# Gate recurrence between the first two heads, the first half of a modulation on TensorE, lambda first, and routing's GpSimd work on VectorE

## Chip, core and metric

One core of a Trainium2 chip runs the whole kernel. The metric is the device time of one execution in microseconds (us). The engines are named PE (TensorE, matmul), PEld (its weight loads), DVE (VectorE), ACT (ScalarE), POOL (GpSimd) and SP (SyncE, which issues most DMAs). SBUF and PSUM are the on-chip memories; P is 128, the number of partitions.

## What is computed

One decoder block for 512 tokens of width 1024, all float32. Cut to what the change touches:

```python
mod = silu(c) @ ada_w + ada_b                      # 1024 -> 6144
sh1, sc1, gt1, sh2, sc2, gt2 = split(mod, 6)
h = rmsnorm(x, norm1_w) * (1 + sc1) + sh1
qa, ka, va, qm, km, vm, om, ip, fp, ga, gm = split_cols(h @ w_in)
lam = exp(sum(lam_q1 * lam_k1)) - exp(sum(lam_q2 * lam_k2)) + lam_init
y_a = diff_attention(qa, ka, va, lam, subln_w)     # 8 heads, softmax(a) - lam * softmax(b)
hm  = mlstm_chunkwise(qm, km, vm, ip, fp)          # gates ip, fp: a recurrence over 8 chunks of 64
x   = x + gt1 * ((sigmoid(ga) * y_a + sigmoid(gm) * rms(hm) * sigmoid(om)) @ w_out)
h2  = rmsnorm(x, norm2_w) * (1 + sc2) + sh2
# product-key routing: 8 heads, two lists of 128 keys each
v_top, i_top = top_k(scores, 16)                   # 16 of each list
cand = v_top[0][:, None] + v_top[1][None, :]       # sums of pairs
cand_idx = i_top[0][:, None] * 128 + i_top[1][None, :]
sc, sel = top_k(cand, 16); idx = cand_idx[sel]; gate = softmax(sc)
x = x + gt2 * sum_e gate_e * gelu(U[idx_e] . h2) * V[idx_e]   # 16384 experts
return rmsnorm(x, final_norm_w)
```

## The kernel before

The kernel is written in Python on a framework that puts each engine's instructions in a fixed order at build time; on the chip each engine runs its list in order, with semaphores between engines. Buffers come from pools with a fixed number of slots (`bufs`), and an instruction that wants a slot waits for its last reader. Products in float32 precision are made of three matmuls: an operand is split in a rounded part (hi, a cast on ACT) and a rest (lo, a subtraction on DVE or POOL).

1. **Start**, to about 70 us. `ada_early(half)` loads 16 tiles of `ada_w` (128x512) for each half of the columns of sh1 and sc1, and DVE adds each, times the condition vector, to an accumulator (`ada_step`, lines 217 and 219); `ada_cols` (line 224) sums it over the partitions with one-column matmuls against ones and adds the bias (line 225). sh1 and sc1 make hT (hi on ACT, line 291; lo on DVE, line 293), the input of all projections; the projections q and k of the first two heads and the gates are multiplied first (line 187 and below). Behind that stands the lambda chain (lp, ls, le, nl, psl).
2. **Heads**, to about 690 us. Four passes `hp` of two heads each: `attention(hp)` with two heads `u`, `mlstm(hp)`, and the gates om, gm, ga (line 682). In pass 0 `gate_chain()`, the recurrence over the forget gates on 8 partitions, stands behind `attention(0)`.
3. **Routing**, about 697 to 1005 us. For three of the four token tiles: `scores` and `top16` (lines 747 to 751), `select` (line 772: pair sums cand on DVE and cidx on POOL; per head a comparison eq, 128x800, on DVE, its product oh with cidx on POOL, the sum idxf on DVE), `slots` (transposes; expert index taken apart by shift and mask), and `build_w`: for each of 48 batches of 8 tokens two one-hot tensors n2T, n1T and two gated ones ghi, glo (line 844, 128x1024 f16 each), from which PE makes the dense weights W (wps, lines 852 and 853). Six of the 48 glo are made on POOL (`PLO`). Meanwhile the first experts' products `up(n1)` run ahead, by up to 32 (`NGA`): raw_U is loaded, hi_U cast on ACT (line 966), lo_U subtracted (line 967: POOL for n1 < 35, else DVE), a one-column copy `pace` on POOL (line 969) and 24 act matmuls of 128x384 (lines 975 to 977).
4. **Main loop**, about 1013 to 1960 us. n1 from 0 to 127, 128 experts in each: `up(n1)`, the load and split of V (hi_V, lo_V), ga times W (line 1006), its split ahi and alo, and 18 y matmuls of 128x512 (line 1021). The fourth token tile is routed inside this loop by `select_gather` (at n1 = 3 and 5) and served by indirect DMAs (gath) from POOL, with DVE adding up (lines 907 and 917).

Of the kernel before, what the change touches and what calls it, by code (L numbers as in the profile page):

```python
# [1108 lines left out]
```

## Time and profile before

| | us |
|---|---|
| median of 3 runs (1979.67 to 1980.06) | 1979.73 |
| the profiled execution, its own time | 1986.29 |
| its span in the trace | 1984.2 |
| PE busy | 1826.5 (92%) |
| DVE busy | 1465.3 (74%) |
| POOL busy | 861.2 (43%) |
| ACT busy | 806.8 (41%) |

The profile is of one execution; its busy times are of the whole span and average over stages that are unlike. Windows give the same by stage. Where an instruction is in a group, "idle before" is the time its engine stood still ahead of it, with the event that ended it.

### The profile page before, as it was taken

What the parts mean: (1) busy time and instruction counts of PE and PEld (TensorE: products, weight loads), DVE (VectorE), ACT (ScalarE), POOL (GpSimd) and SP (SyncE); (2) the same over time, 40 slices, a digit from 0 to 9 for tenths busy, and PEclk for the clock granted to TensorE, in tenths of its full rate; (3) what the DMA queues carried; (4) which work ended last, traced back from release to release, by engine and by line L of the source; (5) the groups of instructions that cost most, each with busy time, mean ns of one, the idle gap of its engine ahead of it and who ended that gap; (6) DMA issues with size and microseconds to landing.
All of it is one profiled execution on the core that took longest, in us unless ns stands there. A gap on an engine that the chain in (4) does not pass through costs nothing.

```text
span 1984.2 us, 29045 instructions
## 1 busy us (share of the span) xinstructions
PE 1826.5 (92%) x10748; PEld 1648.0 (83%) x10748; DVE 1465.3 (74%) x2740; ACT 806.8 (41%) x1361; POOL 861.2 (43%) x721
## 2 busy tenths in 40 slices
PE   5989999899997988778899989999999999999997
PEld 4979899798986877678888778889988888888986
DVE  7653646546557799998999878888777677767777
ACT  4545464464553323344444333333333333332332
POOL 2513425234234256675533556555433423333433
PEclk8999999999998999899899999999999999999998
DMA  7321414324223222255596699999978888887983
GB/s 278 123 64 60 149 65 154 113 67 139 64 86 107 86 90 81 85 183 202 203 312 215 216 331 339 334 345 348 337 253 296 293 283 291 288 299 234 320 290 129
DMA packets 160284, 404.27 MB, mean 204 GB/s; under 512 B 14471, under 2 KB 63368, under 8 KB 160142
## 3 DMA queue, kind: packets, MB, share of 16 engines
q1 hardware_dynamic: 117026, 240.91, 37.2%
q0 software_dynamic: 36864, 134.23, 18.6%
q10 hardware_dynamic: 6252, 27.28, 3.6%
q8 instruction: 84, 1.38, 0.3%
q14 instruction: 58, 0.48, 0.1%
HBM read 373.52 MB, written 28.84 MB: 203 GB/s over the span
## 4 chain that ended last, share of the span: by engine, by line
PE 51%; DVE 23%; DMA 10%; issue 6%; POOL 5%; ACT 4%; SPq 0%; DVEq 0%; POOLq 0%; ACTq 0%
PE y L1021 18%; PE act L977 5%; PE act L975 5%; PE act L976 5%; DMA ada_w<-ada_w 4%; DMA gath<-V,idx 3%; DVE onehot L844 3%; DVE gated L844 2%; DVE lo_V L138 1%; DVE lo_U L967 1%; DVE eq L797 1%; DMA gath<-U,idx 1%; POOL gath L901 1%; DVE idxf L800 1%; ACT hi_U L966 1%
## 5 line engine op out<-in xcount | busy, mean ns | idle before, releaser
L977 PE MATMUL act<-h_hi,lo_U 128*128 128x384 f32 x1024 | 353.9, 346 | 14.7 <-POOL lo_U L967 9.7
L975 PE MATMUL act<-h_hi,hi_U 128*128 128x384 f32 x1024 | 351.5, 343 | 1.9 <-ACT ga L979 1.9
L976 PE MATMUL act<-h_lo,hi_U 128*128 128x384 f32 x1024 | 350.7, 342 | 0.0
L917 DVE SCALAR_TENSOR_TENSOR yg<-gath,act,yg 128x1024 f32<-128x1024 f32 x127 | 162.9, 1283 | 110.3 <-DMA gath<-V,idx 109.6
L1021 PE MATMUL y<-lo_V,ahi 128*128 128x512 f32 x762 | 238.9, 394 | 5.5 <-DVE lo_V L138 5.5
L1021 PE MATMUL y<-hi_V,alo 128*128 128x512 f32 x762 | 234.1, 394 | 4.0 <-DVE alo L138 4.0
L1021 PE MATMUL y<-hi_V,ahi 128*128 128x512 f32 x762 | 222.1, 396 | 7.3 <-ACT hi_V L137 7.3
L901 POOL DMA_INDIRECT gath<-U,idx x128 | 176.6, 1380 | 115.3 <-DVE junk L907 101.1
L137 ACT CAST hi_V<-raw_V 128x1024 fp32r<-128x1024 f32 x128 | 134.1, 1051 | 225.6 <-PE y L1021 197.1
L977 PEld LDWEIGHTS act<-h_hi,lo_U 128*128 128x128 f32 x1024 | 197.0, 192 | 22.4 <-POOL lo_U L967 11.1
L969 POOL COPY pace<-lo_U 128x1 f32<-128x1 f32 x128 | 69.9, 548 | 331.6 <-DVE lo_U L967 330.1
L975 PEld LDWEIGHTS act<-h_hi,hi_U 128*128 128x128 f32 x1024 | 197.8, 193 | 10.8 <-ACT ga L979 3.1
L976 PEld LDWEIGHTS act<-h_lo,hi_U 128*128 128x128 f32 x1024 | 197.5, 193 | 3.6
L137 ACT CAST ahi<-ga 128x384 fp32r<-128x384 f32 x127 | 65.1, 513 | 302.2 <-DVE ga L1006 152.1
L138 DVE TENSOR_TENSOR lo_V<-raw_V,hi_V 128x1024 fp32r<-128x1024 f32 x128 | 158.0, 1236 | 33.2 <-ACT hi_V L137 30.6
L966 ACT CAST hi_U<-raw_U 128x1024 fp32r<-128x1024 f32 x128 | 134.1, 1048 | 110.0 <-PE act L976 92.3
L1021 PEld LDWEIGHTS y<-hi_V,alo 128*128 128x128 f32 x762 | 143.5, 189 | 35.9 <-DVE alo L138 5.2
L1021 PEld LDWEIGHTS y<-lo_V,ahi 128*128 128x128 f32 x762 | 142.7, 189 | 36.7 <-DVE lo_V L138 7.9
L1021 PEld LDWEIGHTS y<-hi_V,ahi 128*128 128x128 f32 x762 | 143.0, 190 | 32.1 <-ACT hi_V L137 8.0
L901 POOL DMA_INDIRECT gath<-V,idx x128 | 152.5, 1192 | 38.0 <-issue 30.2
L907 DVE SCALAR_TENSOR_TENSOR junk<-gath,hrow 128x1024 bf16<-128x1024 f32 x128 | 156.1, 1220 | 11.9 <-DMA gath<-U,idx 11.2
L967 POOL TENSOR_TENSOR lo_U<-raw_U,hi_U 128x1024 fp32r<-128x1024 f32 x35 | 105.0, 3001 | 72.5 <-ACT hi_U L966 59.1
(461 smaller groups left out, 4413.1 us busy)
## 6 DMA issues: line engine op xcount, KB each, us to landing
raw_U<-UT SPq DMA_DIRECT2D x128, 512.0 KB, 5.1
raw_V<-V SPq DMA_DIRECT2D x128, 512.0 KB, 5.0
ada_w<-ada_w SPq DMA_DIRECT2D x96, 256.0 KB, 4.0
W_dram<-st ACTq DMA_DIRECT2D x24, 960.0 KB, 4.5
...
```

The lines of the kernel that those rows point to most:

```text
L137: A.copy(hi, src)
L138: eng.tensor_tensor(lo, src, hi.bitcast(F32), op=OP.subtract)
L844: eng.tensor_tensor(dst.rearrange("p t (n u) -> p t n u", u=2), x.rearrange("p t (n u) -> p t n u", u=2), bc(y[:, b * TB:(b + 1) * TB, Non ...
L901: G.indirect_dma_start(out=t_, out_offset=None, in_=src, in_offset=bass.IndirectOffsetOnAxis(ap=idx0[:, s:s + 1], axis=0))
L907: V.scalar_tensor_tensor(junk2, u, 1.0, hrow, op0=OP.mult, op1=OP.mult, accum_out=act[:, s:s + 1])
L917: V.scalar_tensor_tensor(yg, v, act[:, s:s + 1], yg, op0=OP.mult, op1=OP.add)
L966: A.copy(hi, raw)
L967: (G if n1 < NGA + 3 else V).tensor_tensor(lo, raw, hi.bitcast(F32), op=OP.subtract)
L975: T.matmul(ps, hi[:, ks], h_hi[:, k], start=(k == 0), stop=False)
L976: T.matmul(ps, hi[:, ks], h_lo[:, k], start=False, stop=False)
L977: T.matmul(ps, lo[:, ks], h_hi[:, k], start=False, stop=(k == KD - 1))
L1021: T.matmul(ys[d][j], l[:, tsl], r[:, j * 512:(j + 1) * 512], start=(m == 0 and i == 0), stop=(m == KEYS - 1 and i == 2))
```

## The change

Five things change.

1. The 16 `ada_w` tiles of the first half are no longer multiplied on DVE; PE multiplies each (condition column as the stationary operand, one row of 512 results, added up in PSUM), ACT copies the row, and `ada_cols` then uses one row. The second half stays on DVE.
2. The lambda chain is written at the very start, and the load of its four vectors second in SP's queue.
3. `gate_chain` is called between the two heads of pass 0, not behind them.
4. `select` finds both key indices by comparing the position with the 16 offsets of the pair list, on DVE in f16 alone, for four heads in one instruction; POOL makes neither cidx nor oh, and `slots` needs no shift and mask. In `build_w` the two one-hot operations become one of 128x2048, and all glo are made on DVE.
5. lo_U is made on DVE always (line 967 before, 994 after).

```diff
+    def ada_cols(acc, n, b0, dst, rows=P):
...
-            T.matmul(ps[:, k:k + 1], acc[:, k * P:(k + 1) * P], ones[:, 0:1], start=True, stop=True)
+            T.matmul(ps[:, k:k + 1], acc[0:rows, k * P:(k + 1) * P], ones[0:rows, 0:1], start=True, stop=True)
+    lamv = load_const("lamv", [1, 4, 64], a["lamv"])
+    lq = ftile([1, 2, 64], F32, "lp")
...
+    A.activation(le, ls, AF.Exp)
...
@@ ada_early(half)
+                ps = acc_tile(f"ada_row{i}")[0:1] if half == 0 else None
...
-                    ada_step(accs[i][:, hs], w, k)
+                    if half == 0:
+                        T.matmul(ps, cond[:, k:k + 1], w, start=(k == 0), stop=(k == KD - 1))
+                    else:
+                        ada_step(accs[i][:, hs], w, k)
+                if half == 0:
+                    A.copy(accs[i][0:1, hs], ps)
...
@@ attention and its caller
         for u in range(2):
+            if u and between:
+                between()
...
-        attention(hp, y_a, ssq[:, 0])
-        if hp == 0:
-            gate_chain()
+        attention(hp, y_a, ssq[:, 0], gate_chain if hp == 0 else None)
...
@@ select
-        for h in range(n):
-            eq, oh = mk("eq", [P, TOPK, NC], F16), mk("oh", [P, TOPK, NC])
-            sh = [P, TOPK, NC // 2, 2]
-            V.tensor_tensor(eq.rearrange("p k (c u) -> p k c u", u=2), bc(pos2[:, h, :, None, :], sh),
-                            bc(iota_c.rearrange("p (c u) -> p c u", u=2)[:, None], sh), op=OP.is_equal)
-            G.tensor_tensor(oh, eq, bc(cidx[:, h, None, :], [P, TOPK, NC]), op=OP.mult)
-            V.tensor_reduce(didx[:, h], oh, axis=AX.X, op=OP.add)
...
+        each_pos(ge, off_c, OP.is_ge)
+        of_head(st[:, 0:n * TOPK], ge, di)
+        V.tensor_tensor(st[:, n * TOPK:], ge, bc(doff_c[:, None, :], [P, n * TOPK, TOPK]), op=OP.mult)
+        V.tensor_reduce(two.rearrange("p a q -> p (a q)"), st, axis=AX.X, op=OP.add)
+        V.tensor_copy(dn1, two[:, 0].rearrange("p (h k) -> p h k", k=TOPK))
+        V.tensor_tensor(pos2, pos2, bc(two[:, 1, :, None], [P, n * TOPK, 2]), op=OP.subtract)
+        eq = mk("ge", [P, n * TOPK, TOPK], F16)
+        each_pos(eq, iota_c, OP.is_equal)
+        of_head(eq, eq, ij[:, 1])
+        V.tensor_reduce(dn2, eq.rearrange("p (h k) c -> p h k c", h=n), axis=AX.X, op=OP.add)
...
@@ build_w
-            each(e2, iota_rep, n2T, OP.is_equal)
-            each(e1, iota_rep, n1T, OP.is_equal)
-            each(r_hi, e1, ghi, OP.mult)
-            each(r_lo, e1, glo, OP.mult, G if b % 8 < PLO else V)
+            V.tensor_tensor(pairs[0].rearrange("p a t (n u) -> p (a t) n u", u=2),
+                            iota_rep.rearrange("p t (n u) -> p t n u", u=2),
+                            bc(n21T[:, b].rearrange("p a t u -> p (a t) u")[:, :, None, :], [P, 2 * TB, KEYS // 2, 2]),
+                            op=OP.is_equal)
...
@@ up(n1)
-        (G if n1 < NGA + 3 else V).tensor_tensor(lo, raw, hi.bitcast(F32), op=OP.subtract)
+        V.tensor_tensor(lo, raw, hi.bitcast(F32), op=OP.subtract)
```

The order of instructions on an engine shows where these land. On DVE at the start, before: ada_acc_131 and 132 are accumulators, adac the column sums of the first half.

```order
L219 SCALAR_TENSOR_TENSOR ada_acc_132<-ada_w,cond,ada_acc_132 128x512
L225 TENSOR_TENSOR sh_106<-adac_346,adabT 128x4
L181 TENSOR_TENSOR lo_q_0_185<-raw_q_0_183,hi_q_0_184 128x1024
L225 TENSOR_TENSOR sc_107<-adac_352,adabT 128x4
L217 TENSOR_SCALAR ada_acc_131<-ada_w,cond 128x512
L289 SCALAR_TENSOR_TENSOR sc_107<-sc_107,n1w 128x4
```

On DVE at the same place, after: the accumulators 145 and 146 are now those of the second half.

```order
L217 TENSOR_SCALAR ada_acc_145<-ada_w,cond 128x512
L219 SCALAR_TENSOR_TENSOR ada_acc_145<-ada_w,cond,ada_acc_145 128x512 x7
L217 TENSOR_SCALAR ada_acc_146<-ada_w,cond 128x512
L219 SCALAR_TENSOR_TENSOR ada_acc_146<-ada_w,cond,ada_acc_146 128x512
L226 TENSOR_TENSOR sh_106<-adac_363,adabT 128x4
L219 SCALAR_TENSOR_TENSOR ada_acc_146<-ada_w,cond,ada_acc_146 128x512
L226 TENSOR_TENSOR sc_107<-adac_369,adabT 128x4
L219 SCALAR_TENSOR_TENSOR ada_acc_146<-ada_w,cond,ada_acc_146 128x512
L311 SCALAR_TENSOR_TENSOR sc_107<-sc_107,n1w 128x4
```

Ten steps of the second half now stand ahead of sh of the first half, and two more between sh and the finished sc.

On ACT around the gate recurrence (iw, R) and the evacuation of om, before; a_hi, oT and junk_s are of the second head.

```order
L137 CAST a_hi<-aTp 128x4x128
L504 COPY oT<-po 128x512
L510 ACTIVATE junk_s,ssq<-pt,rinv 128x128 x3
L355 ACTIVATE iw<-iw 8x512
L356 ACTIVATE R<-R 8x512
L682 ACT_TABLE_LOAD
L682 ACTIVATE om<-pt_om_0_1483 128x512
L682 ACTIVATE om<-pt_om_1_1533 128x512
```

On ACT, after; oT and junk_s are of the first head, qz opens the second.

```order
L513 COPY oT<-po 128x512
L362 ACTIVATE iw<-iw 8x512
L363 ACTIVATE R<-R 8x512
L519 ACTIVATE junk_s,ssq<-pt,rinv 128x128
L364 ACTIVATE R<-an 8x512
L689 ACT_TABLE_LOAD
L689 ACTIVATE om<-pt_om_0_1487 128x512
L370 CAST part<-M 8x512
L519 ACTIVATE junk_s,ssq<-pt,rinv 128x128
L538 ACT_TABLE_LOAD
L538 ACTIVATE kT_m<-cv 128x512
L519 ACTIVATE junk_s,ssq<-pt,rinv 128x128 x2
```

The recurrence and the first om evacuation now stand between the heads; the second om evacuation follows some rows below, ahead of the second head's first cast.

On DVE in the one-hot building, before: eq and idxf are the selection of the next token tile, between the batches.

```order
L844 TENSOR_TENSOR onehot<-iota_6507,n1T 128x1024
L844 TENSOR_TENSOR gated<-onehot,ghi 128x1024
L844 TENSOR_TENSOR gated<-onehot,glo 128x1024
L800 TENSOR_REDUCE idxf_6518<-oh 128x16
L797 TENSOR_TENSOR eq<-pos_8824,iota_c 128x800
```

On DVE in the one-hot building, after; lo_U is the rest of an expert tile for `up`.

```order
L994 TENSOR_TENSOR lo_U_10908<-raw_U_10906,hi_U_10907 128x1024
L868 TENSOR_TENSOR onehot<-iota_6512,n21T 128x2048 x2
L872 TENSOR_TENSOR gated<-onehot,ghi 128x1024
L874 TENSOR_TENSOR gated<-onehot,glo 128x1024
L872 TENSOR_TENSOR gated<-onehot,ghi 128x1024
L874 TENSOR_TENSOR gated<-onehot,glo 128x1024
L868 TENSOR_TENSOR onehot<-iota_6512,n21T 128x2048
L994 TENSOR_TENSOR lo_U_10978<-raw_U_10976,hi_U_10977 128x1024
L872 TENSOR_TENSOR gated<-onehot,ghi 128x1024
L874 TENSOR_TENSOR gated<-onehot,glo 128x1024
L994 TENSOR_TENSOR lo_U_11049<-raw_U_11047,hi_U_11048 128x1024
```

The lo_U, which were in POOL's list, stand in DVE's between the one-hot operations, one to about two batches. In the whole order DVE has 36 of them between the first top-16 and the last gated product; 14.1 ups' matmuls stand on PE ahead of the first wps (before: 9), 34 ahead of the first y matmul (before: 33.1), and the last 13 batches of wps have no act matmul between them. ACT has 55 table loads (before: 49).

## Rows read from the trace of the kernel before

**Rows 1.** The page: the span, and the busy share of VectorE (DVE) in tenths, in 40 equal slices of the span.

```profile
span 1984.2 us, 29045 instructions
...
DVE  7653646546557799998999878888777677767777
```

**Rows 2.** Windows of the span: stretch and length in us, busy us of each engine with its instructions, the granted clock of TensorE as a share, the busy share of the DMA engines, GB/s. The first two are the routing stage, the last is the main loop.

```profile
697.00:806.00 109.00, 89.70 (x443) 79.00 (x442) 105.33 (x547) 37.81 (x71) 70.88 (x91) 0.94 0.28 87
806.00:1005.00 199.00, 165.00 (x1339) 155.21 (x1338) 184.65 (x222) 85.37 (x144) 121.09 (x63) 0.90 0.52 183
...
1150.00:1960.00 810.00, 797.21 (x3933) 713.28 (x3934) 615.47 (x752) 280.99 (x385) 361.84 (x328) 0.99 0.86 300
```

**Rows 3.** Groups of DVE instructions from 697 to 1005 us, shapes apart: line, operation, out<-in, shapes and count | busy us, mean ns of one | idle us ahead of them and what ended it.

```profile
L844 DVE TENSOR_TENSOR onehot<-iota,n2T 128x1024 f16<-128x1024 f16 x48 | 51.0, 1067 | 12.6 <-PE wps L853 12.6
L844 DVE TENSOR_TENSOR gated<-onehot,ghi 128x1024 f16<-128x1024 f16 x48 | 47.2, 990 | 0.2
L844 DVE TENSOR_TENSOR onehot<-iota,n1T 128x1024 f16<-128x1024 f16 x48 | 45.7, 955 | 0.0
L844 DVE TENSOR_TENSOR gated<-onehot,glo 128x1024 f16<-128x1024 f16 x42 | 34.6, 824 | 0.0
L797 DVE TENSOR_TENSOR eq<-pos,iota_c 128x800 f16<-128x800 f16 x24 | 24.1, 1015 | 0.0
L800 DVE TENSOR_REDUCE idxf<-oh 128x16 f32<-128x800 f32 x24 | 23.2, 968 | 0.0
...
L783 DVE TENSOR_TENSOR cand<-vals 128x64 f32<-128x64 f32 x6 | 7.5, 1255 | 0.0
...
L807 DVE TENSOR_TENSOR gates<-ex,esm 128x64 f32<-128x64 f32 x6 | 4.2, 692 | 0.0
```

**Rows 4.** All instructions of one kind of lines 844 (in the same stretch) and 797: count, minimum, median and maximum duration in ns, first and last start in us.

```profile
L844 DVE TENSOR_TENSOR onehot<-iota,n2T x48: 675/682/2879, 813.4 to 998.7; 128x1024 f16<-128x1024 f16 x48
...
L797 DVE TENSOR_TENSOR eq<-pos,iota_c x24: 549/588/2428, 717.1 to 861.8; 128x800 f16<-128x800 f16 x24
```

**Rows 5.** Timeline of DVE and then of GpSimd (POOL) from 887 to 896 us: start us, duration us, instruction.

```profile
887.29 0.68 DVE L844 TENSOR_TENSOR onehot<-iota,n1T 128x1024 f16<-128x1024 f16 x1
888.00 2.27 DVE L844 TENSOR_TENSOR gated<-onehot,ghi 128x1024 f16<-128x1024 f16 x1
890.19 2.83 DVE L844 TENSOR_TENSOR gated<-onehot,glo 128x1024 f16<-128x1024 f16 x1
892.94 2.85 DVE L844 TENSOR_TENSOR onehot<-iota,n2T 128x1024 f16<-128x1024 f16 x1
...
889.68 5.56 POOL L967 TENSOR_TENSOR lo_U<-raw_U,hi_U 128x1024 fp32r<-128x1024 f32 x2
```

**Rows 6.** Groups of POOL instructions from 697 to 1005 us, columns as in rows 3.

```profile
L967 POOL TENSOR_TENSOR lo_U<-raw_U,hi_U 128x1024 fp32r<-128x1024 f32 x33 | 99.7, 3022 | 69.5 <-ACT hi_U L966 56.1 <-issue 7.8 <-ACT W L858 5.1
L799 POOL TENSOR_TENSOR oh<-eq,cidx 128x800 f32<-128x800 f16 x24 | 45.6, 1907 | 25.7 <-DVE eq L797 19.1 <-DVE n2T L828 4.5 <-DVE vals L750 0.9
...
L138 POOL TENSOR_TENSOR lo_wq<-raw_wq,hi_wq 128x1024 fp32r<-128x1024 f32 x4 | 9.6, 2396 | 1.7 <-ACT hi_wq L137 1.6
```

**Rows 7.** All lo_U of the execution that DVE makes, columns as in rows 4.

```profile
L967 DVE TENSOR_TENSOR lo_U<-raw_U,hi_U x93: 1199/1222/1228, 1040.4 to 1945.0; 128x1024 fp32r<-128x1024 f32 x93
```

**Rows 8.** Timeline of DVE, then of TensorE (PE), where the routing stage hands over to the main loop. Columns as in rows 5, with the idle time ahead of an instruction and what ended it.

```profile
1002.77 0.69 DVE L844 TENSOR_TENSOR gated<-onehot,glo 128x1024 f16<-128x1024 f16 x1
1005.97 3.35 DVE L138 TENSOR_TENSOR lo_V<-raw_V,hi_V 128x1024 fp32r<-128x1024 f32 x2 [2.51 <-PE wps L853]
1009.24 5.10 DVE L1006 TENSOR_TENSOR ga<-ga,W 128x384 f32<-128x384 f32 x6
...
1012.71 0.34 PE L977 MATMUL act<-h_hi,lo_U 128*128 128x384 f32 x1
1012.88 0.33 PE L975 MATMUL act<-h_hi,hi_U 128*128 128x384 f32 x1
...
1013.23 0.63 PE L1021 MATMUL y<-hi_V,ahi 128*128 128x512 f32 x2
```

**Rows 9.** Three windows behind the first two attention heads (columns as in rows 2), and one row of the table of waits from 120 to 165 us (engine and line that waited, for what: us in total, times, longest).

```profile
130.00:140.00 10.00, 5.51 (x26) 3.63 (x26) 8.54 (x19) 4.99 (x17) 0.46 (x1) 0.87 0.31 107
140.00:150.00 10.00, 4.86 (x18) 3.40 (x16) 5.76 (x21) 2.86 (x9) 0.00 (x0) 0.67 0.00 0
150.00:160.00 10.00, 7.22 (x41) 7.22 (x42) 2.79 (x6) 8.67 (x14) 4.63 (x3) 0.60 0.05 13
...
PE pt_gm L187 <- ACT om L682: 6.6, 1, 6.6
```

**Rows 10.** The start. Timeline of DVE, of ACT and of PE; then the two forms of the ada_w steps on DVE and the matmuls of line 395 on PE (columns as in rows 4).

```profile
25.79 2.50 DVE L217 TENSOR_SCALAR ada_acc<-ada_w,cond 128x512 f32<-128x512 f32 x1
...
28.46 2.93 ACT L291 ACTIVATE hT_hi<-xT,sh,sc 128x512 fp32r<-128x512 f32 x4 [2.96 <-DVE sc L289]
...
45.91 1.41 PE L224 MATMUL adac<-ones,ada_acc 128*128 128x1 f32 x6 [3.10 <-DVE nl L320]
...
L219 DVE SCALAR_TENSOR_TENSOR ada_acc<-ada_w,cond,ada_acc x28: 731/752/753, 11.5 to 45.0; 128x512 f32<-128x512 f32 x28
L217 DVE TENSOR_SCALAR ada_acc<-ada_w,cond x4: 473/482/2495, 10.8 to 35.1; 128x512 f32<-128x512 f32 x4
...
L395 PE MATMUL adar<-ada_acc,ones x8: 589/593/697, 338.8 to 497.9; 128*128 128x512 f32 x8
```

More of the change, by code (lines that the diff above doesn't have):

```diff
@@ L37 @@
 NC = sum(PAIRS)
+OFFS = [sum(PAIRS[:i]) for i in range(TOPK)]
 PIECES = [c for hp in range(4) for c in (
@@ L44 @@
 QB = 1
-PLO = 1
 RB = 6
@@ L733, in block_kernel @@
     rp = rx.enter_context(tc.tile_pool(name="routep", bufs=1, side="right"))
-    n1T, n2T, ghi, glo = [rp.tile([P, XT, 2], F16, name=n) for n in ("n1T", "n2T", "ghi", "glo")]
+    n21T = rp.tile([P, XT // TB, 2, TB, 2], F16, name="n21T")
+    ghi, glo = [rp.tile([P, XT, 2], F16, name=n) for n in ("ghi", "glo")]
     iota16 = rp.tile([P, KEYS], F16, name="iota16")
@@ L738, in block_kernel @@
     V.tensor_copy(iota16, jcol)
-    iota_rep = bc(iota16[:, None, :], [P, TB, KEYS])
-    V.tensor_copy(iota_c, jcol[:, 0:NC])
+    iota_rep = bc(iota16[:, None, :], [P, 2 * TB, KEYS])
+    V.tensor_copy(iota_c, jcol[:, 0:TOPK])
+    for i in range(TOPK):
+        G.memset(off_c[:, i:i + 1], float(OFFS[i]))
+        G.memset(doff_c[:, i:i + 1], float(OFFS[i] - OFFS[max(i - 1, 0)]))
     vals, inds = [{t: rp.tile([P, 2, NH, TOPK], dt, name=f"{n}{t}") for t in DBS}
                   for n, dt in (("vals", F32), ("inds", U32))]
-    idxf, gates = [{t: rp.tile([P, NH, TOPK], F32, name=f"{n}{t}") for t in DBS} for n in ("idxf", "gates")]
+    picks = {t: rp.tile([P, 3, NH, TOPK], F32, name=f"picks{t}") for t in DBS}
     def top16(src, scratch, v, i):
@@ L809, in mk_rp @@
     def mk_rp(name, shape, dt=F32):
-        return rp.tile(shape, dt, tag=name, bufs=2, name=name)
+        return rp.tile(shape, dt, tag=name, bufs=1 if name == "stp" else 2, name=name)
     def select_dense(t, h0, n):
         hs = slice(h0, h0 + n)
-        select(vals[t][:, :, hs], inds[t][:, :, hs], n, mk_rp, idxf[t][:, hs], gates[t][:, hs])
+        select(vals[t][:, :, hs], inds[t][:, :, hs], n, mk_rp, *[picks[t][:, i, hs] for i in range(3)])
     def slots(t):
         cs = slice((t - DBS[0]) * P, (t - DBS[0] + 1) * P)
+        bs = slice((t - DBS[0]) * P // TB, (t - DBS[0] + 1) * P // TB)
         ps = tr_tile("slots")
-        T.transpose(ps[:, 0:P], idxf[t].rearrange("p h k -> p (h k)"), ident)
-        T.transpose(ps[:, P:2 * P], gates[t].rearrange("p h k -> p (h k)"), ident)
-        ii = rp.tile([P, TOPK * NC], I32, tag="oh", bufs=2, name="ii")[:, 0:3 * P].rearrange("p (a b) -> p a b", b=P)
-        V.tensor_copy(ii[:, 0], ps[:, 0:P])
-        V.tensor_scalar(ii[:, 1], ii[:, 0], 7, None, op0=OP.logical_shift_right)
-        V.tensor_scalar(ii[:, 2], ii[:, 0], KEYS - 1, None, op0=OP.bitwise_and)
-        pair = [P, P, 2]
-        V.tensor_copy(n1T[:, cs], bc(ii[:, 1, :, None], pair))
-        V.tensor_copy(n2T[:, cs], bc(ii[:, 2, :, None], pair))
-        gp = bc(ps[:, P:2 * P, None], pair)
+        for i in range(3):
+            T.transpose(ps[:, i * P:(i + 1) * P], picks[t][:, i].rearrange("p h k -> p (h k)"), ident)
+        for i in range(2):
+            src = ps[:, i * P:(i + 1) * P].rearrange("p (b t) -> p b t", t=TB)
+            V.tensor_copy(n21T[:, bs, 1 - i], bc(src[:, :, :, None], [P, P // TB, TB, 2]))
+        gp = bc(ps[:, 2 * P:3 * P, None], [P, P, 2])
         V.tensor_scalar(ghi[:, cs], gp, GS, None, op0=OP.mult)
```

95 lines of the change are left out of this document (51 added, 44 removed).

## Prediction

> **What bounds the kernel now.** First the span and its slices [rows 1]: VectorE's (DVE's) busy share lies between 3 and 7 tenths in the first third of the span and stands at 8 or 9 from the fifteenth slice (of 49.6 us each) to the twenty-second, so another engine than TensorE (PE) may set the time there. The windows [rows 2] say so by stage. In the main loop, 1150 to 1960, PE is busy for 797 of 810 us and DVE for 615: PE sets the time, and an edit that only saves DVE or GpSimd (POOL) work there is worth nothing. In the routing stage, 697 to 1005, DVE is busy for 105.3 + 184.7 = 290.0 of 308 us and PE for 89.7 + 165.0 = 254.7: DVE sets the time, and PE would allow at most 53 us less.
>
> Then what DVE does in that stage [rows 3]. The four groups of one-hot operations (128x1024 f16) take 178 us of the 290, eq and idxf of the selection 47. Their means are 0.82 to 1.07 us, but the list of minimum, median and maximum [rows 4] has a median of 0.682 us and a maximum of 2.88 us for one and the same shape (eq: 0.588 and 2.43): some run at full speed, some stand. The timeline [rows 5] shows which: at 888 to 895.7 three in a row take 2.27, 2.83 and 2.85 us, and in just that stretch POOL runs two lo_U (and ends a gated product); the operation ahead of them takes 0.68. So DVE pays for what POOL does at the same time. POOL's groups of the stage [rows 6] are lo_U (99.7 us, 33 of them), oh (45.6), 4 lo_wq (9.6) and, by the code, 6 gated products.
>
> **The routing stage.** The change takes oh and the index sums, the 6 gated products and all lo_U away from POOL; only the 4 lo_wq stay. The time lost by DVE today is mean minus median: n2T 48 x (1067 - 682) = 18.5 us, ghi 48 x (990 - 682) = 14.8, n1T 48 x (955 - 682) = 13.1, glo 42 x (824 - 682) = 6.0, eq 24 x (1015 - 588) = 10.2. For the 128x64 sums (1255) and gates (692) I take 0.30 as undisturbed, an estimate from 0.68 us for sixteen times as many f16 elements, so 5.7 and 2.4. Sum 70.7 us. Four lo_wq of 2.4 us each leave some of it: at most 9.6, I take 6.
>
> There the Trainium skill bears on the case: "SBUF — State Buffer", section "SBUF: two separate sides", says that DVE and GpSimd share a pair of ports by an exclusive lock for a whole instruction, so that the other engine blocks fully. By that rule the four lo_wq would hold DVE for the whole 9.6 us and the sum would be 3.6 us worse; the trace's stretch of 2.27 to 2.85 us for operations of 0.68 agrees with it in kind.
>
> What comes onto DVE. A lo_U on DVE takes 1.222 us in the late loop [rows 7], and consecutive DVE instructions overlap by 0.08 us (890.19 against 888.00 + 2.27, [rows 5]), so 1.14 each. By the order, 36 lo_U stand between the first top-16 and the last gated product on DVE: 36 x 1.14 = 41.0. Six gated products at 0.60: 3.6. The selection is run six times here: in each, five f16 operations of 1024 elements (5 x 0.60 = 3.0) and reductions of 2048 and 1024 elements at the rate of idxf (968 ns for 800: 2.5 + 1.2), some 0.5 for small copies, 7.2 in all, against four eq and four idxf of 0.51 and 0.89 = 5.6 today: 6 x 1.6 = 9.6 more. The merged one-hot (2048 instead of twice 1024) saves one fixed part in each of 48; from 800 elements in 0.588 and 1024 in 0.682 us that is between nothing and 0.19 us, so 0 to 9 us; I take 4, since two sizes are a short base. The new broadcast f16 operations aren't in the trace: below, the rate of a one-hot (0.60), above, that of an f32 subtraction (1.14), which would add 30 x 0.54 = 16 us. I take 0.60, since all five have f16 operands and the form of the one-hots.
>
> DVE: 290.0 - 70.7 + 6 + 41.0 + 3.6 + 9.6 - 4 = 275.5. Idle today 18 us, 12.6 of it waiting for wps ahead of n2T [rows 3]; with half as many one-hot starts, and with new waits of lo_U for hi_U, I take 10: 285.5 instead of 308, **-22**. Ends: -43 (no idle, no lo_wq loss, 6 + 10 + 5 more) and -6 (f16 at the f32 rate).
>
> The moved lo_U brings a wait: in DVE's list a lo_U that waits for ACT's hi_U holds up the one-hots behind it, and wps on PE behind those. On POOL these 33 stood idle for 69.5 us in all, 56.1 of it for hi_U [rows 6]; there nothing else waited. The order places one lo_U after some 3.5 to 4.7 us of DVE work, and PE needs 24 x 0.17 = 4.1 us for the matmuls of one (spacing in [rows 8]), so hi_U, freed by these matmuls, is about as often ready as wanted. Hence my 10 us of idle, not 0.
>
> **The hand-over to the loop.** DVE ends its one-hots at 1003.5 and the first y matmul is at 1013.2; between them lo_V (two in 3.35 us) and ga (six in 5.10 us) [rows 8], while POOL runs its last lo_U. At full speed two lo_V take 2.4. PE does act matmuls in those 10 us, which are work for the loop anyway; by the order the changed kernel has 34 ups done ahead of the first y, not 33.1, at 4.1 us each: -3.7. I take **-4** (0 to -8).
>
> **Between the first two heads.** From 130 to 160 us PE is busy for 5.51, 4.86 and 7.22 us in three windows of 10, at a granted clock of 0.87, 0.67 and 0.60 [rows 9]: at full clock that is 5.51 x 0.87 + 4.86 x 0.67 + 7.22 x 0.60 = 12.4 us of work, 17.6 lost. PE's wait is the one for om (6.6 us): ACT's om evacuations stand behind both heads and behind the start of the gate recurrence, and PE's next projection wants the accumulator. With the recurrence between the heads, its chain over DVE, ACT and POOL runs while PE multiplies om, and om's evacuation stands ahead of the second head, whose matmuls fill PE when the chain is done. Six more table loads by the order come onto ACT, which is busy for 5.0 and 2.9 us of 10 in the first two of the windows. I take two thirds, **-12** (0 to -18); 0 if the second head's scores on ACT wait as long as mLSTM does now.
>
> **The start.** The 16 tiles of the first half leave DVE (14 x 0.752 and 2 x 0.48 us) for PE, which waits there; at the price of an adar matmul (128x512) of 0.593 us they are 9.5 us, and each waits for its DMA as before. But the DMA sets when they end, and by the order ten steps of the second half (0.7 each, spacing) stand on DVE ahead of sh, sc and so of hT_hi, which now starts at 28.46 [rows 10]: the first projections come 4 to 6 us later. The second half's steps end 4 to 6 us earlier in return, as does the wait for them (adac waits 3.1 us behind lambda's nl, which is gone from there). POOL's lo_q, which today stretches the L217 to 2.50 us, stays. I take **-2** (-4 to +4).
>
> **Sum.** -22 - 4 - 12 - 2 = -40. The sums are made on the profiled execution (1986.29 us by its time, 1984.2 by its span); the median of the runs is 1979.73, 6.6 below, and I take the saving off the median: **1940 us**.
>
> **Rivals.** (1) DVE inherits POOL's waits: all 69.5 us [rows 6] come into DVE's queue, with one-hots behind: 1940 + 70 = 2010, slower. It decides from 40 us on, 1.1 us for each of 36 lo_U. For it: the same hi_U on ACT, also queued behind W0's evacuation. Against it: POOL's own lo_U took 3.02 us and sat between ACT and PE, so each next hi_U came late through it; at 1.22 that loop is 1.8 us shorter. Chance 0.06. (2) The stretched operations don't come from POOL: then none of the 65 us returns, 2005; [rows 5] speak against it, 0.03. (3) The loop gives back what routing wins, by gathers or loads that come too soon: only start and heads stay, -14, 1966. For it the DMA share of 0.86, against it PE's 797 of 810 [rows 2]. 0.10. (4) New f16 operations at the f32 rate, or no gain between the heads: -24 to -28, 1952 to 1956. 0.15. (5) Everything comes in full: -43 - 4 - 18 - 2 = -67, 1913. 0.09. The forecast's own case, 1926 to 1951, has 0.57.
>
> **Range and chances.** From 1914 (case 5) to 1966 (case 3); outside are cases 1 and 2 and half of 5, some 0.14, a little more with unknown edges. A change of 0.2%, 4 us, is about the least that can be told from none here. Faster by more: cases 3 to 5 and the forecast, 0.91; within: 0.02; slower: 0.07.
>
> **What would show it.** The one-hot of 2048 near 1.2 us and the gated near 0.68 in nearly all instances, with a tail only beside lo_wq; DVE idle ahead of lo_U below 10 us; first y some 40 us sooner than 1013; PE full from 130 to 160 with no pt_gm wait; hT_hi starting after 32. Wrong it goes if DVE's idle before lo_U reaches 40 us, if the reductions or broadcasts take twice my price, or if the second head waits for the recurrence.

## The result, and the profile after

The changed kernel takes 1930.55 us (median, 1928.49 to 1936.19), against 1979.89 in the runs beside it: a ratio of 0.9751 (0.9727 to 0.9775), 49.3 us less. The profiled execution of after has 1931.38 us, a span of 1929.6, and lies at its median; that of before lies 6.4 us above its own. The two spans therefore differ by 54.6 us, and some 5 of these belong to the execution of before, not to the change.

Five marks that stand in both programs cut the span (us, starts in the trace):

| mark | before | after | difference | gained since the mark above |
|---|---|---|---|---|
| first gate matmul (start) | 29.4 | 36.0 | +6.6 | |
| first v projection | 70.0 | 72.2 | +2.2 | 4.4 |
| first query projection pr_wq of routing | 637.1 | 628.4 | -8.7 | 10.9 |
| first y matmul | 1013.2 | 966.6 | -46.6 | 37.9 |
| last act matmul h_hi, hi_U of the loop | 1950.3 | 1898.0 | -52.3 | 5.7 |

The page first: VectorE's (DVE's) slices of 9 end with the twentieth (of 48.2 us each), where [rows 1] had them up to the twenty-second (of 49.6 us).

```profile
span 1929.6 us, 28952 instructions
...
DVE  5564746646556799999988888887777767767677
```

The windows of the routing stage, the start of the main loop and the loop (columns as in rows 2): from 688 to 963 us DVE is busy for 267.6 of 275 us, against 290.0 of 308 [rows 2]; TensorE (PE) is now busy for 254.3 of 275.

```profile
688.00:763.00 75.00, 67.81 (x338) 57.50 (x337) 73.74 (x372) 22.63 (x42) 10.53 (x8) 0.98 0.31 97
763.00:814.00 51.00, 47.64 (x273) 46.22 (x272) 50.31 (x218) 22.65 (x34) 3.25 (x10) 1.00 0.36 107
814.00:963.00 149.00, 138.90 (x1257) 129.60 (x1255) 143.54 (x184) 82.29 (x140) 53.29 (x22) 0.95 0.66 238
...
1100.00:1900.00 800.00, 792.30 (x3905) 703.40 (x3904) 610.02 (x744) 276.58 (x378) 354.61 (x328) 1.00 0.87 304
```

The groups of DVE from 688 to 963 us (columns as in rows 3). The gated operations have a mean of 0.685 us, against 0.990 and 0.824 [rows 3], and lo_U waits 0.6 us in all for hi_U, not the 56.1 us that it waited for it on GpSimd (POOL) [rows 6].

```profile
L868 DVE TENSOR_TENSOR onehot<-iota,n21T 128x2048 f16<-128x2048 f16 x48 | 57.4, 1220 | 2.8 <-PE wps L879 2.8
L994 DVE TENSOR_TENSOR lo_U<-raw_U,hi_U 128x1024 fp32r<-128x1024 f32 x36 | 43.7, 1215 | 1.0 <-ACT hi_U L993 0.6 <-issue 0.4
L872 DVE TENSOR_TENSOR gated<-onehot,ghi 128x1024 f16<-128x1024 f16 x48 | 32.7, 685 | 0.2
L874 DVE TENSOR_TENSOR gated<-onehot,glo 128x1024 f16<-128x1024 f16 x48 | 32.7, 685 | 0.0
L822 DVE TENSOR_REDUCE two<-stp 128x128 f32<-128x2048 f16 x6 | 13.6, 2265 | 0.0
...
L828 DVE TENSOR_REDUCE picks<-ge 128x64 f32<-128x1024 f16 x6 | 7.2, 1204 | 0.0
```

Minimum, median and maximum of the one-hot (columns as in rows 4): no tail is left, where [rows 4] had a maximum of four times the median.

```profile
L868 DVE TENSOR_TENSOR onehot<-iota,n21T x48: 1207/1218/1228, 805.2 to 958.8; 128x2048 f16<-128x2048 f16 x48
```

The groups of POOL in the same stretch (columns as in rows 6): copies of one column that wait for DVE, and the four lo_wq.

```profile
L996 POOL COPY pace<-lo_U 128x1 f32<-128x1 f32 x36 | 57.4, 1601 | 160.2 <-DVE lo_U L994 160.2
L138 POOL TENSOR_TENSOR lo_wq<-raw_wq,hi_wq 128x1024 fp32r<-128x1024 f32 x4 | 9.7, 2420 | 44.8 <-ACT hi_wq L137 44.6 <-PE pkeys L777 0.2
```

Between the heads, the three windows of rows 9: PE is busy for 7.8, 10.0 and 9.6 of 10 us, not 5.5, 4.9 and 7.2, at clocks of 0.97, 0.85 and 1.00, and there is no wait of pt_gm for om any more.

```profile
130.00:140.00 10.00, 7.81 (x63) 7.26 (x62) 6.16 (x6) 7.47 (x10) 7.89 (x5) 0.97 0.20 63
140.00:150.00 10.00, 10.00 (x67) 9.05 (x67) 6.44 (x14) 8.43 (x21) 1.50 (x2) 0.85 0.15 57
150.00:160.00 10.00, 9.63 (x80) 9.08 (x78) 4.82 (x10) 7.96 (x15) 4.74 (x2) 1.00 0.24 60
```

The start, from the timeline: PE's last run of ada_row, the adac matmuls behind the transposes, and the first hT_hi on ScalarE (ACT), which stood at 28.46 [rows 10].

```profile
20.29 7.03 PE L263 MATMUL ada_row<-ada_w,cond 128*1 128x512 f32 x16
...
31.24 1.94 PE L225 MATMUL adac<-ones,ada_acc 1*128 1x1 f32 x16 [0.18 <-ACT xT L295]
...
35.06 2.93 ACT L313 ACTIVATE hT_hi<-xT,sh,sc 128x512 fp32r<-128x512 f32 x4 [3.38 <-DVE sc L311]
```

All ada_row matmuls (columns as in rows 4): 16 in the code, 32 on the engine.

```profile
L263 PE MATMUL ada_row<-ada_w,cond x32: 591/592/1061, 10.0 to 26.7; 128*1 128x512 f32 x32
```

The hand-over, from DVE's timeline: two lo_V in 2.36 and six ga in 2.89 us, against 3.35 and 5.10 [rows 8].

```profile
960.63 0.68 DVE L874 TENSOR_TENSOR gated<-onehot,glo 128x1024 f16<-128x1024 f16 x1
963.21 2.36 DVE L138 TENSOR_TENSOR lo_V<-raw_V,hi_V 128x1024 fp32r<-128x1024 f32 x2 [1.90 <-PE wps L879]
965.49 2.89 DVE L1033 TENSOR_TENSOR ga<-ga,W 128x384 f32<-128x384 f32 x6
```

### The profile page after: what moved, and what is told of

Its sections match the earlier page's. It is cut to its first block, busy times and chain, and to the rows that moved or that the text cites. A ratio compares the mean times of both kernels' runs of the same rounds, so it can differ in the third digit from the quotient of the medians.

```text
span 1929.6 us, 28952 instructions
## 1 busy us (share of the span) xinstructions
PE 1832.0 (95%) x10783; PEld 1631.9 (85%) x10783; DVE 1421.9 (74%) x2732; ACT 814.0 (42%) x1361; POOL 694.7 (36%) x608
## 4 chain that ended last, share of the span: by engine, by line
PE 59%; DVE 18%; DMA 8%; ACT 6%; issue 5%; POOL 3%; SPq 0%; DVEq 0%; POOLq 0%; ACTq 0%
PE y L1048 22%; PE act L1004 6%; PE act L1002 6%; PE act L1003 6%; DMA gath<-V,idx 5%; DVE lo_U L994 2%; DMA ada_w<-ada_w 2%; POOL gath L927 1%; DVE lo_V L138 1%; ACT hi_U L993 1%; DVE ga L706 1%; DVE ada_acc L219 1%; ACT p L496 1%; PE ada_row L263 1%; PE wps L879 1%
## 5 line engine op out<-in xcount | busy, mean ns | idle before, releaser
L1004 PE MATMUL act<-h_hi,lo_U 128*128 128x384 f32 x1024 | 346.6, 339 | 7.3 <-DVE lo_U L994 7.1
L1002 PE MATMUL act<-h_hi,hi_U 128*128 128x384 f32 x1024 | 345.2, 337 | 5.8 <-ACT ga L1006 5.0
L1003 PE MATMUL act<-h_lo,hi_U 128*128 128x384 f32 x1024 | 344.2, 336 | 0.0
L996 POOL COPY pace<-lo_U 128x1 f32<-128x1 f32 x128 | 107.9, 845 | 570.9 <-DVE lo_U L994 570.7
L1048 PE MATMUL y<-lo_V,ahi 128*128 128x512 f32 x762 | 243.2, 399 | 4.6 <-DVE lo_V L138 4.6
L1004 PEld LDWEIGHTS act<-h_hi,lo_U 128*128 128x128 f32 x1024 | 192.2, 188 | 15.9 <-DVE lo_U L994 11.7
L1002 PEld LDWEIGHTS act<-h_hi,hi_U 128*128 128x128 f32 x1024 | 192.4, 188 | 12.3 <-ACT ga L1006 6.2
L1003 PEld LDWEIGHTS act<-h_lo,hi_U 128*128 128x128 f32 x1024 | 192.3, 188 | 4.0
L1048 PEld LDWEIGHTS y<-hi_V,alo 128*128 128x128 f32 x762 | 143.4, 189 | 35.8 <-DVE alo L138 1.6
L994 DVE TENSOR_TENSOR lo_U<-raw_U,hi_U 128x1024 fp32r<-128x1024 f32 x128 | 156.0, 1219 | 19.9 <-ACT hi_U L993 16.9
```

Of the source, the lines that this page charges most:

```text
L994: V.tensor_tensor(lo, raw, hi.bitcast(F32), op=OP.subtract)
L996: with tc.issue_after(G.tensor_copy(pace, lo[:, 0:1].bitcast(F32)).ins):
L1002: T.matmul(ps, hi[:, ks], h_hi[:, k], start=(k == 0), stop=False)
L1003: T.matmul(ps, hi[:, ks], h_lo[:, k], start=False, stop=False)
L1004: T.matmul(ps, lo[:, ks], h_hi[:, k], start=False, stop=(k == KD - 1))
L1048: T.matmul(ys[d][j], l[:, tsl], r[:, j * 512:(j + 1) * 512], start=(m == 0 and i == 0), stop=(m == KEYS - 1 and i == 2))
```

## The experiments

The theory: DVE, which bounds routing, pays for two-input POOL operations that run at the same time; the gain there is these pauses less the work that DVE takes over. The main rivals: POOL cost time by its place in the chain from raw_U to the act matmuls, or the new selection alone was the gain. DVE's busy time (pauses are in it, since a stretched operation counts as busy) and its idle time tell the first two apart.

Marks of all runs in us, from each profiled execution, in the order of the text, which calls a run by its number. "Routing" is from the first pr_wq to the first y, "loop" from there to the last mark of the table above.

| run | median | first gate | first v | first pr_wq | routing | loop |
|---|---|---|---|---|---|---|
| before | 1979.9 to 1983.6 | 29.4 | 70.0 | 637.1 | 376.1 | 937.1 |
| changed | 1930.6 | 36.0 | 72.2 | 628.4 | 338.2 | 931.4 |
| e5_loU_on_dve_only | 1967.5 | 28.2 | 65.8 | 635.5 | 353.5 | 942.7 |
| e3_loU_on_pool | 1949.1 | 36.8 | 73.2 | 627.2 | 358.9 | 923.1 |
| e4_pool_dummy | 1985.3 | 37.1 | 73.4 | 627.5 | 388.6 | 934.0 |
| e7_pool_copy_dummy | 1944.8 | 36.3 | 72.5 | 626.2 | 347.6 | 929.7 |
| e6_onehot_split | 1930.6 | 35.7 | 71.9 | 625.4 | 343.6 | 929.5 |
| e8_small_ops_on_act | 1932.3 | 29.3 | 69.2 | 626.9 | 338.2 | 933.8 |
| e1_heads_only | 1971.0 | 28.2 | 67.3 | 625.2 | 376.0 | 934.1 |
| e2_ada_on_dve | 1921.5 | 29.0 | 67.5 | 624.5 | 339.1 | 924.3 |
| e11_ada_on_dve_again | 1929.6 | 29.0 | 69.0 | 630.1 | 338.5 | 926.3 |
| e10_changed_again | 1931.1 | 35.8 | 72.0 | 625.6 | 340.4 | 932.0 |
| e9_half_mod_split | 1948.2 | 35.0 | 74.2 | 631.6 | 340.4 | 941.8 |

The loop's length ranges from 923.1 to 942.7 us. The same kernel run twice agrees far better (changed and e10: 931.4 and 932.0; e2 and e11: 924.3 and 926.3), so most of this lies between kernels. In all of them PE is busy for 914 to 922 us of it; the other 7 to 28 us are waits, for lo_U, lo_V, hi_V and ahi, and no run shows what sets them. Routing differs by 2.2 us between the two executions of the changed kernel. Differences of a few us in the median are therefore read at the marks, not at the end.

**lo_U alone, and all but lo_U.** The first (e5) makes the fifth point of the change alone, in the kernel before; the second (e3) undoes it alone, in the changed one.

> The kernel before, with only lo_U of n1 < 35 moved from POOL to DVE; selection, one-hots, heads and start are as before. My theory: DVE takes over 41 us of lo_U, loses some 45 us of standing beside POOL's lo_U, and the hand-over to the main loop is no longer stretched; together with the 18.5 us that the same move is worth in the changed kernel, 1960 to 1973 us. Rival of the prediction (DVE inherits POOL's 69.5 us of waiting for hi_U): 1995 to 2015.

> The changed kernel with lo_U of n1 < 35 back on POOL. By the theory that DVE pays for POOL's operations: DVE is rid of 41 us of lo_U in the routing stage, but one-hot and gated operations show a tail of 2 to 3 us again and lose 40 to 55 us; PE's act matmuls wait for lo_U again; 1935 to 1950 us. Rival (the gain came from the new selection, and lo_U on DVE cost its 41 us): faster than the changed kernel, 1895 to 1925 us.

Measured: 1967.5 us, ratio to before 0.9932 (0.9905 to 0.9958), and 1949.1 us, 0.9846 (0.9829 to 0.9864), both within what the theory gave. With two changes on and off, routing takes 376.1 (neither), 353.5 (lo_U moved), 358.9 (all the rest of the change), 338.2 (both): moving lo_U is worth 22.6 us before and 20.7 in the changed kernel, the rest 17.2 and 15.3. The two add up within 2 us. Of the rest, only the merged one-hot has a run of its own (e6); the new selection and the six glo were not tried apart. With lo_U on POOL the tail is back, minimum, median and maximum of the gated operation:

```profile
L872 DVE TENSOR_TENSOR gated<-onehot,ghi x48: 674/680/2883, 809.2 to 979.3; 128x1024 f16<-128x1024 f16 x48
```

And where DVE makes lo_U in the kernel before, its waits in routing hold no entry for hi_U at all; the largest and that of the one-hots (engine and line, for what: us in total, times, longest):

```profile
DVE lo_wq L138 <- ACT hi_wq L137: 1.6, 1, 1.6
...
DVE onehot L844 <- PE wps L853: 0.6, 1, 0.6
```

That settles the prediction's first rival. The windows of the stage, of e5 and then of e3 (columns as in rows 2), say how much is pauses:

```profile
695.00:986.00 291.00, 258.22 (x1860) 236.91 (x1858) 286.64 (x805) 129.71 (x221) 136.99 (x124) 0.95 0.49 165
687.00:982.00 295.00, 258.46 (x1862) 237.53 (x1861) 281.99 (x736) 126.63 (x214) 137.63 (x74) 0.95 0.46 161
```

With lo_U back on POOL (e3), DVE is busy for 14.4 us more than in the changed kernel and idle for 13.0 instead of 7.4. With lo_U moved in the kernel before (e5), its busy time falls by only 3.4 us, from 290.0 to 286.6, as the lo_U that it takes over nearly use up the pauses that go; its idle time falls from 18.0 to 4.4, and another 5 us go between the last gated product and the first y. So POOL's place in the chain did cost time as well. One-hots waited 12.6 us for wps in the kernel before [rows 3] and 0.6 in e5, 10.0 in e3 and 2.8 in the changed kernel; wps stand on PE behind act matmuls, which waited 9.7 and 7.4 us for POOL's lo_U in the kernel before and in e3.

**POOL work that nothing reads.** Two further operations on POOL for each of the 35 tiles, in the changed kernel.

```diff
+        if n1 < NGA + 3:
+            for c in range(2):
+                dmy = dp.tile([P, 512], F32, tag="dmy", bufs=1, name="dmy")
+                G.tensor_tensor(dmy, raw[:, c * 512:(c + 1) * 512], hi.bitcast(F32)[:, c * 512:(c + 1) * 512], op=OP.subtract)
```

> The changed kernel with, per expert tile of n1 < 35, two further subtractions on POOL (128x512 f32, raw_U minus hi_U, into a scratch tile that nothing reads). Nothing waits for them but the slots of raw_U and hi_U. By the theory that DVE pays for what POOL does beside it: the one-hot and gated operations beside them stand, some 21 tiles x 2.5 us of POOL at 0.6 to 0.8 each, 25 to 45 us slower, 1955 to 1975. Rival (POOL cost time in the kernel before only by standing in the chain from raw_U to the act matmuls): 1929 to 1935, one-hot at 1.22 throughout.

To make room for the scratch tile, this run and the next also give the tile ge, which DVE alone writes and reads, one slot instead of two.

Measured: 1985.3 us, ratio to before 1.0029 (1.0016 to 1.0043); routing is 50.4 us longer than in the changed kernel. The sign is the theory's, the size is above its upper end. The timeline shows one such pair: two one-hots take 4.54 us beside it, the gated ahead and behind 0.68.

```profile
882.62 0.68 DVE L874 TENSOR_TENSOR gated<-onehot,glo 128x1024 f16<-128x1024 f16 x1
...
883.17 3.50 POOL L998 TENSOR_TENSOR dmy<-raw_U,hi_U 128x512 f32<-128x512 f32 x2 [0.43 <-POOL pace L1000]
883.22 4.54 DVE L868 TENSOR_TENSOR onehot<-iota,n21T 128x2048 f16<-128x2048 f16 x2
...
888.67 0.68 DVE L872 TENSOR_TENSOR gated<-onehot,ghi 128x1024 f16<-128x1024 f16 x1
```

The window of the stage (columns as in rows 2), then the 70 subtractions and the gated operation (columns as in rows 4):

```profile
687.00:1012.00 325.00, 268.28 (x1860) 243.35 (x1859) 320.82 (x771) 128.17 (x215) 164.12 (x110) 0.94 0.43 147
...
L998 POOL TENSOR_TENSOR dmy<-raw_U,hi_U x70: 1261/1614/5818, 736.0 to 970.5; 128x512 f32<-128x512 f32 x70
...
L872 DVE TENSOR_TENSOR gated<-onehot,ghi x48: 673/680/1802, 826.4 to 1009.5; 128x1024 f16<-128x1024 f16 x48
```

So 50.4 / 70 = 0.72 us of the stage are lost for each. I had counted only the 21 tiles beside one-hots; the selection's f16 operations and lo_U stand as well (lo_U's mean is 1.432 us here, 1.215 without). Nothing waits for these results, but the slots of raw_U and hi_U do, so a chain over them remains possible. It isn't where the time goes: DVE is busy for 320.8 of 325 us, 53 more than in the changed kernel, and idle for only 4.2 (7.4 there).

**The same with copies.** `G.tensor_copy(dmy, raw[...])` in place of the subtraction.

> As the run with two further subtractions on POOL for each tile of n1 < 35, but the two operations are copies (128x512 f32, one input, raw_U) into the scratch tile. If any POOL operation that reads SBUF holds DVE's two-input operations up for its duration: DVE's one-hot and gated show a tail again, as long as a copy, 1940 to 1965 us. If only two-input subtractions on POOL do it: 1929 to 1934, no tail.

Measured: 1944.8 us (1937.2 to 1949.8), 0.9828 (0.9798 to 0.9858), within the first range; in the profiled execution, the fastest, routing is 9.4 us longer. The copies and the gated operation:

```profile
L998 POOL COPY dmy<-raw_U x70: 610/801/10941, 731.8 to 931.3; 128x512 f32<-128x512 f32 x70
...
L872 DVE TENSOR_TENSOR gated<-onehot,ghi x48: 672/678/1103, 810.1 to 967.2; 128x1024 f16<-128x1024 f16 x48
```

A copy with one input also holds DVE up. The longest stretch of a gated product (maximum less median) goes with what POOL runs beside it: 2.20 us beside lo_U (e3), which takes POOL at least 2.34; 1.12 beside the subtractions, at least 1.26; 0.43 beside the copies, at least 0.61. The loss is 0.13 us of the stage for each copy, against 0.72 for each subtraction: one-input work on POOL isn't free beside DVE, and here it cost less even for the time that it takes.

**One one-hot of 2048 or two of 1024.**

```diff
-            V.tensor_tensor(pairs[0].rearrange("p a t (n u) -> p (a t) n u", u=2),
...
+            for a_, e_ in enumerate((e2, e1)):
+                V.tensor_tensor(e_.rearrange("p t (n u) -> p t n u", u=2),
+                                iota_rep[:, 0:TB].rearrange("p t (n u) -> p t n u", u=2),
+                                bc(n21T[:, b, a_, :, None, :], sh), op=OP.is_equal)
```

> The changed kernel with the one-hot of 128x2048 made as two of 128x1024. By the fixed part of an instruction, between nothing and 0.19 us for each of 48 (the prediction took 4 us in all): 1931 to 1939 us against 1930.5, DVE's one-hot groups 2 to 8 us longer in sum. If it were the merging that let DVE pass POOL's operations, a tail of 2 to 3 us would come back: over 1945.

The group on DVE from 685 to 966 us:

```profile
L869 DVE TENSOR_TENSOR onehot<-iota,n21T 128x1024 f16<-128x1024 f16 x96 | 61.1, 683 | 2.3 <-PE wps L879 1.9
```

61.1 us against 57.4, and routing 343.6 against 338.2 and 340.4 (the changed kernel, twice), so merging is worth 3 to 5 us there, and no tail comes with the split. The median, 1930.6 us, doesn't show it: the loop was 1.9 us shorter and the stage before 3 us earlier in this kernel.

**Small operations to ACT.** In the kernel of e2, the copies of di and of the first key index, the casts n21T and ghi become ACT instructions.

> The changed kernel with the first half of the modulation back on DVE (1921.5 us) and, in routing, four kinds of small operations moved from DVE to ACT: the copies of the first offset and of the first key index, the two casts n21T and ghi; 7 us of DVE in the stage. If DVE still sets the time there: 1914 to 1919. If PE does by now, or ACT's latency in the chain of the selection eats it: 1920 to 1925.

Measured: 1932.3 us, a miss. Routing is 338.2 us, 0.9 less than in e2, less than the 2.2 by which the changed kernel differs from itself. Some 7 us of instructions were to leave DVE; as they overlap with their neighbours, they took 4.4 us of its time with them. Its one-hots now wait 4.5 us for wps (2.8 in e2), lo_U 2.6 for hi_U (0.6). So most of the work came back as waits for PE and ACT, and by these DVE no longer sets the time of that stage alone. The other 10 us stand in the loop of this kernel (933.8 against 924.3); 5.9 of them are PE's waits for hi_V (6.3 against 0.4).

**The heads alone.** Only `between=gate_chain`, in the kernel before.

> The kernel before, with only the gate recurrence moved between the two heads of pass 0. My theory (the recurrence then lies beside the om projection and the second head's matmuls): PE full from 130 to 160 us, no wait of pt_gm for om, the first projection of pass 1 some 11 us sooner, 1969 us (1966 to 1972), nothing changed behind. Rival (the recovered time came from the earlier lambda or the earlier second half of the modulation): 1978 to 1982.

Measured: 1971.0 us, 0.9938 (0.9913 to 0.9962). The three windows of rows 9:

```profile
130.00:140.00 10.00, 7.81 (x51) 7.22 (x51) 7.59 (x10) 7.17 (x14) 4.69 (x4) 0.83 0.33 118
140.00:150.00 10.00, 10.00 (x77) 8.85 (x76) 7.20 (x15) 8.46 (x19) 1.50 (x2) 1.00 0.04 5
150.00:160.00 10.00, 9.36 (x74) 8.86 (x73) 2.15 (x4) 6.77 (x13) 4.72 (x2) 1.00 0.28 102
```

PE is busy for 7.8, 10.0 and 9.4 us, as in the changed kernel, with lambda where it was. From the first v to the first pr_wq it takes 557.9 us, against 567.1: 9.2 of its gain lie there, and another 2.7 ahead of the first v, which I didn't expect. PE's order is the same up to there; but from 40 to 60 us PE was granted a clock of 0.83 in the execution of before, 0.91 in this one, and 1.00 in that of e5, which leaves the start as it was and reaches the first v at 65.8. So these us look like the execution's, not the edit's.

**The modulation back on DVE.** The first point of the change undone, in the changed kernel.

> The changed kernel with the 16 tiles of the first half back on DVE; lambda stays early. My theory (the PE product delays hT_hi by 6.6 us, because the adac matmuls stand on PE behind the transposes, which stand behind the ada_row products): the first gate matmul is back near 29.5 us and the first v projection (72.2 us in the changed kernel) at or before 70.0, so 1926 to 1929 us against 1930.5. Rival (the delay comes from lamv ahead in SP's queue and the lambda instructions ahead on DVE): the first gate matmul stays after 34 us and the time at 1930 to 1932.

> The changed kernel with the first half of the modulation on DVE once more. The start is worth 4.7 us at the first v projection; the other 4 of the 9 us came from the main loop, where kernels with the same loop differ by up to 10 us. If the start alone is the cause, 3 to 6 us below the changed kernel on this chip; if the difference holds for this build, 8 to 10.

> The changed kernel once more, beside the next run on the same chip: 1928 to 1935 us.

Measured: 1921.5 us first, 9 below the changed kernel, below what I expected; then, beside the changed kernel on one chip, 1929.6 against 1931.1, less of a difference than either case that I had named. The gate is back at 29.0 us in both, so the PE product is what delays it, by 7 us, and not lambda (which stays early here). But at the first pr_wq nothing is left to see: 624.5, 630.1 and (e8) 626.9 with the tiles on DVE; 628.4, 625.6, 627.2, 627.5, 625.4 and 626.2 with them on PE. The heads stage takes 557 to 561 us in the first, 553.5 to 556.2 in the second, so most of the delay is caught up there. Whether the tiles on DVE are 1.5 or 9 us better at the end stays open. What is left lies in the loop, where PE waits for 7.2 and 9.0 us in these two kernels and for 11.3 and 13.8 in the changed one; no run here says why, and in e8, with the tiles on DVE as well, it is 12.9.

**Half of them on PE.** The 8 tiles of sc1 on PE, those of sh1 on DVE.

> The changed kernel with the 16 tiles of the first half shared: the 8 of sh1 on DVE, the 8 of sc1 on PE. My theory of the start (16 tiles on PE are 32 instructions of 0.43 to 0.86 us, from 10.0 to 27.3 us, longer than DVE's 12 us, and the transposes and adac stand behind them): 8 tiles leave PE free near 19 us, the first gate matmul comes at 27 to 31 us, the first v projection at 64 to 68, 1917 to 1924 us. Rival (any PE product of these tiles puts hT_hi behind, because DVE's second-half steps move ahead of sh and sc): gate after 33 us, 1926 to 1931.

Measured: 1948.2 us, 0.9834 (0.9808 to 0.9861), a clear miss. The gate comes at 35.0, as with all 16. The timeline of the start:

```profile
23.86 0.09 PEld L263 LDWEIGHTS ada_row<-ada_w,cond 128*1 128x1 f32 x2 [0.17 <-issue]
...
25.66 5.96 DVE L219 SCALAR_TENSOR_TENSOR ada_acc<-ada_w,cond,ada_acc 128x512 f32<-128x512 f32 x5
...
29.19 1.95 PEld L225 LDWEIGHTS adac<-ones,ada_acc 128*128 128x128 f32 x16 [0.42 <-ACT xT L295]
...
31.54 0.15 DVE L226 TENSOR_TENSOR sh<-adac,adabT 128x4 f32<-128x4 f32 x1
```

PE ends ada_row at 26.6, the transposes that stand between it and adac wait for ACT's evacuations, adac starts at 29.2 and takes 2 us, and DVE's sh stands behind second-half steps until 31.5. So it isn't the length of the PE product alone (my theory), but the order: everything that sh and sc need stands in line behind it. That is nearest to the rival's case, though the line is mostly PE's, not that of DVE's steps, and its time (1926 to 1931) was missed too. Against the changed kernel on the same chip (e10) the median is 17 us longer: 6 lie ahead of the first pr_wq (631.6 against 625.6), none in routing and 10 in the loop, 7 of them waits of PE (21.2 against 13.8).

## Why the prediction was right, and where it was not

The forecast was 1940 (1914 to 1966), faster; 1930.55 was measured, and the case was the forecast's own.

The four terms came out as -34, -4, -11 and +2, so the total is as near as it is in part by luck: the start's miss hides a third of what routing gave more. Two slips changed nothing: the slices of 8 and 9 run to the twenty-third, and case 5 is 1913, not 1914.

**Routing (-22 forecast; -34 to the last wps).** Right in its mechanism: e4 shows the pauses without any data dependence, e3 brings them back, e5 takes the largest share away alone. DVE's busy time in the stage fell by 22.4 us (14.5 forecast), its idle time by 10.6 (8 forecast).

Of the busy time, take each instruction from the end of the one ahead of it, so that an overlap counts once. The terms then came as priced, forecast in brackets: one-hots -35.2 (-35.6 with the merging), gated products -17.2 (-17.2), lo_U +41.0 (+41.0), the new selection less eq and idxf -1.6 (-0.6), the pair sums and gates -7.8 (-8.1); 1.5 more went in small operations that weren't counted. Within the selection the reductions were cheaper (2.27 and 1.20 us, against 2.5 and 1.2) and the small copies dearer (6.5 us in all by their durations, against 3). The mis-sized term is the 6 us added for pauses beside the four lo_wq: they cost some 3 us (1.10 for a gates product of else 0.21, 1.56 for a copy of else 0.19, and two smaller ones), which stand in the terms above already. They are so few since lo_wq runs mostly beside the top-16 search. The timeline shows two of the four:

```profile
726.94 2.26 DVE L822 TENSOR_REDUCE two<-stp 128x128 f32<-128x2048 f16 x1
...
727.75 2.40 POOL L138 TENSOR_TENSOR lo_wq<-raw_wq,hi_wq 128x1024 fp32r<-128x1024 f32 x1 [23.84 <-ACT hi_wq L137]
...
729.13 1.10 DVE L835 TENSOR_TENSOR picks<-ex,esm 128x64 f32<-128x64 f32 x1
...
730.43 2.40 POOL L138 TENSOR_TENSOR lo_wq<-raw_wq,hi_wq 128x1024 fp32r<-128x1024 f32 x1 [0.28 <-ACT hi_wq L137]
...
731.11 0.28 DVE L764 FIND_INDEX8 inds<-vals,scr 128x8 uint32<-128x128 f32 x1
731.31 1.56 DVE L823 COPY picks<-two 128x64 f32<-128x64 f32 x1
```

The reduction (2.26 us) and the one-input search (FIND_INDEX8, 0.28) keep their time, while the gates (1.10) and a copy (1.56) stand.

The idle time was 7.4 us, not 10, with 0.6 us for hi_U. But the reason given for its fall, half as many one-hot starts, is not the one that the runs show: e5, with all the starts of the kernel before, idles 4.4 us, and e3, with half of them, 13.0. The waits went where PE's act matmuls no longer waited for POOL's lo_U.

**Hand-over (-4).** From the last wps to the first y 3.8 us, against 7.6: -3.7. Right: 34.0 ups stand ahead of the first y in the trace, 33.1 before, and lo_V and ga run at full speed.

**Heads (-12).** -10.9 between its marks, -9.2 by e1, with PE full and the wait for om gone. Right; some of the 10.9 is the start's delay caught up, as the runs with the tiles on DVE show.

**Start (-2).** +2.2 at the first v, with the gate 6.6 us later; against e5, whose start is that of before, +6.4. The step that failed is the price of the PE product: "they are 9.5 us". I took one matmul of 0.593 for each tile, but a tile is two instructions, 32 in all, at a spacing of 0.43 us and of 0.86 in the beginning, from 10.0 to 27.3 us. The rows had it: adar's count of 8 [rows 10] belongs to four matmuls of the code. The consequence I had named, hT_hi after 32, came (35.06), but not for the reason given, the ten DVE steps: adac itself starts only at 31.24, against 23.10 before; the steps put sh 2.0 us behind its start (33.24), against 1.1 before.

**The loop.** I expected nothing. The 5.7 us in the two profiles are about as large as one late load in the execution of before, where hi_V waited 9.0 us for raw_V at 1150 and PE 5.9 for hi_V; five of the other runs have such a wait, of 4.3 to 6.3 us. That it is the cause is argued from the size alone. PE's waits for hi_V in the loop, before:

```profile
PE y L1021 <- ACT hi_V L137: 7.3, 2, 5.9
```

and after:

```profile
PE y L1048 <- ACT hi_V L137: 1.2, 1, 1.2
```

The unprofiled runs agree: their medians differ by 49.3 us, near the 46.6 at the first y.

**The lock.** The Trainium skill ("SBUF — State Buffer", section "SBUF: two separate sides") has the exclusive lock only between a GpSimd operation and a DVE operation in a 2-port mode or, if GpSimd's reads SBUF, one with two SBUF inputs. The e4 timeline agrees with it in that two-input DVE operations stand beside a POOL operation with two inputs, and the lo_wq rows in that a one-input search and a reduction don't; which mode the copy that stands has, no run shows. The prediction left that condition out when it set the price by the rule at the 9.6 us of the whole lo_wq; measured were some 3, since little that it covers ran there.
